# A two-layer hybrid decoder step on one core: the small mixer matmuls rewritten to fill the 128x128 array

## The chip, the cores and the metric

The kernel runs on one core of a Trainium2 chip. The metric is the device time of one execution in microseconds. TensorE multiplies matrices (a stationary operand of weights is loaded, a moving operand streams through) and writes PSUM; VectorE and ScalarE do elementwise work; GpSimd here copies and clears small pieces and issues some of the DMAs; SyncE issues the rest.

## The reference

Two layers. Each runs a half-step SwiGLU FFN, a mixer, and a second FFN, on 256 prompt tokens (one sequence) and 32 sample tokens (8 sequences of 4 tokens, each with a state of its own), 288 columns together. A token is 1024 wide.

The mixer projects with `w_in` and runs three branches side by side: retention (4 heads), HGRN2 (8 heads) and RG-LRU; each is normed, gated, projected, gated again and summed. The two that the change touches are:

```
retention: o_t = sum_{s<=t} gamma^(t-s) (q_t . k_s) v_s + (decayed q_t) S_0 ;  S_new = gamma^n S_0 + sum (decayed k_s)^T v_s
HGRN2:     S_t = diag(f_t) S_{t-1} + k_t^T v_t ,  k = 1 - f ,  o_t = S_t^T q_t        (state 128 x 128 per head)
```

Prompt tokens start from a zero state, sample tokens from the given ones. Outputs are the tokens and all new states.

## The kernel before, in words

Everything is held transposed: features on the 128 partitions, the 288 tokens along the columns (256 prompt, the second half reversed, then 32 sample).

**Gemms.** All weights stream in as tiles of 8 x 128 x 128 (`load_w`, on SyncE's queue, five buffers). `split_w` makes two fp32r tiles of each: `wh` by a ScalarE copy, `wl` by a VectorE subtraction. `gemm` (lines 244 to 250) then runs three fp32r matmuls of 288 columns per block: wh x high part, wh x low part, wl x high part. `next_w` keeps up to three units split ahead. A unit has 24 matmuls.

**Mixer.** `PLAN` is a list, written by hand, of which gemm unit comes when. The heads are generators: each `yield` ends a step, and `pump` runs steps of up to two HGRN heads (or one retention head) after each unit, at 1.65 steps a unit. The framework's scheduler then orders instructions on every engine at compile time, by priority and by when it reckons that operands and buffers are free; on the chip each engine follows its list in order. So the small matmuls of the heads stand between gemm matmuls.

**An HGRN head** (`hgrn_head`). Three transposes bring v to token order (`stack_v`). The score matrix `at` over the prompt tokens is built from its diagonal and then by doubling: at half-widths 1, 2, 4, ..., 64 (`LEVELS`), the later half of each block meets the earlier half of it, and q and k are multiplied by the decay of a half (L682, L683).
- Diagonal: two 128x128 products (L636), and one of 32x32 tokens for the samples (L637), masked by the identity (L640, L643).
- Half-widths 1 to 16: `kc` gathers k (ScalarE), one 128x128 product (L670), a masked copy into `at` (L671). At 1 and 2 a further product of 32 stationary columns for the samples (L677), a masked copy into `ats` (L679), and decays on the sample columns (L688, L689).
- Half-width 32: four products of 32 columns each into four strips of partitions; half-width 64: two of 64 (L664). Each is followed by a ScalarE copy into `at`.
- Samples against their states (`sample_mm`): state tiles `st` come by GpSimd's DMA queue (L631, three buffers) and are split into fp32r halves; `qm` holds q block-diagonally (one buffer, cleared once at the start), and 16 fp32r matmuls of 64 stationary columns (L609, L612) accumulate, with one 32x32 fp32 product of the sample scores among them (L611). `sample_out` copies the 64 rows; `fold`, a 64x32 matrix, adds their halves (L710).
- `po` = v x scores (L708, L709), k to token order, the prompt's new state (L731), and the samples' new states: `km` is k masked per sequence (L621), eight matmuls of 128 columns (L739), eight VectorE updates (L742).

**A retention head** (`ret_head`) is alike, with one dense score block (L830, L831, samples L832), two value halves, two state tiles (L820), a mask from DRAM (`dm`, L823), and two folds (L851).

`norms` (L400) multiplies squares by a 128x128 matrix of ones: the sum over partitions appears on all of them.

Of the kernel before, what the change touches and what calls it, by code (L numbers as in the profile page):

```python
# [12 lines left out]
F32 = mybir.dt.float32  # L13
# [37 lines left out]
LEVELS = (1, 2, 4, 8, 16, 32, 64)  # L51

# [47 lines left out]
def tile_hybrid(ctx: ExitStack, tc, i, o):  # L100
# [73 lines left out]
    dsamp = const("dsamp", (TS, RH, TS))  # L174
    lmask = const("lmask", (P, 4, P))
    smask = const("smask", (TS, 2, 16))
# [6 lines left out]
    fold = const("fold", (64, TS))  # L183
    qms = []
    for j in range(1):
        qm = cp.tile([P, NB * 68], F32R, name=f"qm{j}")
        nc.gpsimd.memset(qm.bitcast(F32), 0.0)
        qms.append(qm)
    qmi = [0]
# [240 lines left out]
    def mixer(l, nx):  # L430
# [141 lines left out]
        def replicate(z):  # L572
            zr = small([P, 96], tag="zrep", bufs=3)
# [11 lines left out]
        def stack_v(z, zr, vT, vs, v1):  # L585
            pt = tokens(z, zr)
            act(vT, pt[:, : 2 * P].rearrange("p (c d) -> p c d", c=2), AF.Copy)
            act(vs, pt[:TS, 2 * P : 3 * P], AF.Copy)
# [3 lines left out]
        def sample_q(qs):  # L592
            qm = qms[0]
# [4 lines left out]
            
# [4 lines left out]
        def sample_mm(pq, j, sp, ats, vs):  # L603
            qm = qms[0]
            dv = slice(j * P, (j + 1) * P)
            for b in range(NB):
# [12 lines left out]
        def bmasked(k1):  # L619
            km = small([96, NB, P], F32R, tag="km", bufs=1)  # L620
            tt(km, k1.bitcast(F32).unsqueeze(1).broadcast_to((96, NB, P)),  # L621
# [4 lines left out]

        def hgrn_head(h, f, k, q, qt, zv, zr):
            vT, vs = vtiles()
# [3 lines left out]
            stack_v(zv, zr, vT, vs, v1)  # L632
            pd = mixps()
            for c in range(2):
                b0 = c * P
# [3 lines left out]
            ats = small([TS, TS], tag="ats", bufs=3)  # L639
# [3 lines left out]
            tt(ats, pd[:TS, TP:T], ident[:TS, :TS], ALU.mult)  # L643
# [3 lines left out]
            for li, hw in enumerate(LEVELS):  # L647
                if hw > 1:
                    yield
                if hw == 2 * DS:  # L650
                    pq = mixps()
                    sample_mm(pq, 0, sp, ats, vs)
                    os_ = sample_out(pq, P)
                w = T if hw < DS else TP
# [4 lines left out]
                pl = mixps()  # L659
                if hw >= 32:  # L660
                    for b in range(nb):
                        s0, c = b * hw, b % 2
                        t0 = s0 - hw if c else s0 + hw
                        mm(pl[s0 : s0 + hw, :hw], k[:, c * P + s0 : c * P + s0 + hw],  # L664
                           qt[:, c * P + t0 : c * P + t0 + hw], start=True, stop=True)
                        act(at[s0 : s0 + hw, c * TP + t0 : c * TP + t0 + hw], pl[s0 : s0 + hw, :hw], AF.Copy)
                else:
                    kc = small([P, P], tag="kc", bufs=1)
                    act(kc.rearrange("p (n c j) -> p n c j", c=2, j=hw), kv, AF.Copy)
                    mm(pl[:, :P], kc, qv, start=True, stop=True)  # L670
# [3 lines left out]
                        pl[:, :P].rearrange("p (n c j) -> p n c j", c=2, j=hw))  # L674
                if hw < DS:
                    rv = qt[:, TP:].rearrange("p (n u j) -> p n u j", u=2, j=hw)[:, :, 1, :]
                    mm(pl[:TS, P : P + 16], k[:, TP:], rv, start=True, stop=True)  # L677
                    av = ats.rearrange("p (n u j) -> p n u j", u=2, j=hw)[:, :, 1, :]
                    nc.vector.copy_predicated(  # L679
                        av, smask[:, li, :].rearrange("p (n j) -> p n j", j=hw).bitcast(U32),  # L680
# [446 lines left out]
```

## Time and profile before

| | |
|---|---|
| time, median of 3 runs | 1956.81 us (1953.67 to 1957.28) |
| span of the profiled execution, first to last instruction | 1951.3 us |
| TensorE matmul, busy | 1922.3 us (99%), 14456 instructions |
| TensorE weight load, busy | 1859.4 us (95%) |
| VectorE | 1343.6 us (69%), 2532 instructions |
| ScalarE | 1095.2 us (56%), 1987 instructions |
| GpSimd | 78.7 us (4%) |
| granted TensorE clock | 0.998 of full speed |
| DMA moved | 318.40 MB, mean 163 GB/s |

The profiled execution has no other time than its span; what lies around the span is the distance to the median of the runs, 5.5 us. How to read it: engines run beside each other, so the busy times don't add up. Ends of matmuls are modelled and overlap, so that the distance between starts tells more than a duration. A line such as L664 is a line of the kernel before; `mix` is a PSUM tile of the mixer, `acc` one of a gemm, `w` a general work tile.

### The profile page before, as it was taken

To read this page: it belongs to the slowest core of one execution; us is meant where nothing else is said; L and a number is where in the kernel's file an instruction comes from. 1 tells how busy PE (TensorE), PEld (TensorE's weight loads), DVE (VectorE), ACT (ScalarE), POOL (GpSimd) and SP (SyncE) were. 2 spreads that over 40 slices of the span, in tenths; PEclk is the share of its full clock that TensorE was granted. 3 is DMA by queue.
4 is the path that set the end of the run, shared out by engine and by line. 5 is a ranking of instruction groups with operands and counts; after the bars stand their busy time and mean duration, and the time that the engine had idled before them with its cause. 6 is when DMAs were issued, how large, how long until landed. Compare 5 with 4: busy or idle time off the path is not lost.

```text
span 1951.3 us, 36645 instructions
## 1 busy us (share of the span) xinstructions
PE 1922.3 (99%) x14456; PEld 1859.4 (95%) x14456; DVE 1343.6 (69%) x2532; ACT 1095.2 (56%) x1987; POOL 78.7 (4%) x206
## 2 busy tenths in 40 slices
PE   8999999999999999999999999999999999999998
PEld 7999998999999999999999999899999999999997
DVE  6665678776677767665566657787766776776654
ACT  7444487656665565444444445775657646654443
POOL 2000022000000000000000001210000000000000
PEclk9999999999999999999999999999999999999999
DMA  7555445635544455555555554445355444555553
GB/s 268 164 167 162 144 143 177 202 112 184 199 143 157 137 189 164 163 171 159 168 171 164 165 165 151 166 153 175 133 185 182 141 137 139 170 166 163 169 163 94
DMA packets 94875, 318.40 MB, mean 163 GB/s; under 512 B 11280, under 2 KB 17360, under 8 KB 94704
## 3 DMA queue, kind: packets, MB, share of 16 engines
q1 hardware_dynamic: 87552, 293.74, 47.0%
q0 software_dynamic: 6576, 21.73, 3.3%
q8 instruction: 114, 1.87, 0.4%
q10 hardware_dynamic: 576, 0.59, 0.1%
q14 instruction: 57, 0.47, 0.1%
HBM read 295.67 MB, written 20.35 MB: 162 GB/s over the span
## 4 chain that ended last, share of the span: by engine, by line
PE 91%; DVE 4%; ACT 3%; issue 1%; POOL 1%; DMA 0%; SPq 0%; DVEq 0%; POOLq 0%; ACTq 0%
PE acc L248 22%; PE acc L249 22%; PE acc L250 22%; PE acc L350 5%; PE acc L351 5%; PE acc L349 5%; PE mix L670 1%; PE mix L664 1%; ACT wh L123 1%; PE mix L612 1%; DVE wl L234 1%; ACT chunk L123 1%; PE mix L609 1%; PE mix L581 1%; PE mix L400 1%
## 5 line engine op out<-in xcount | busy, mean ns | idle before, releaser
L248 PE MATMUL acc<-chunk,wh 128*128 128x288 f32 x3456 | 1037.8, 300 | 8.8 <-ACT wh L123 6.6
L249 PE MATMUL acc<-chunk,wh 128*128 128x288 f32 x3456 | 1024.1, 296 | 0.0
L250 PE MATMUL acc<-chunk,wl 128*128 128x288 f32 x3456 | 1019.1, 295 | 2.4 <-DVE wl L234 2.4
L123 ACT ACTIVATE wh<-wr 128x1024 fp32r<-128x1024 f32 (+2 forms) x531 | 553.1, 1042 | 718.9 <-PE acc L249 357.1
L234 DVE TENSOR_TENSOR wl<-wr,wh 128x1024 fp32r<-128x1024 f32 (+2 forms) x531 | 637.7, 1201 | 264.4 <-ACT wh L123 247.8
L248 PEld LDWEIGHTS acc<-chunk,wh 128*128 128x128 f32 x3456 | 650.2, 188 | 13.0 <-ACT wh L123 8.9
L250 PEld LDWEIGHTS acc<-chunk,wl 128*128 128x128 f32 x3456 | 649.6, 188 | 4.9 <-DVE wl L234 4.1
L249 PEld LDWEIGHTS acc<-chunk,wh 128*128 128x128 f32 x3456 | 650.3, 188 | 3.5 <-DVE chunk L263 0.3
L349 PE MATMUL acc<-chunk,wh 128*128 128x288 f32 x704 | 206.9, 294 | 0.0
L350 PE MATMUL acc<-chunk,wh 128*128 128x288 f32 x704 | 206.9, 294 | 0.0
L351 PE MATMUL acc<-chunk,wl 128*128 128x288 f32 x704 | 206.9, 294 | 0.0
L350 PEld LDWEIGHTS acc<-chunk,wh 128*128 128x128 f32 x704 | 132.1, 188 | 0.0
L351 PEld LDWEIGHTS acc<-chunk,wl 128*128 128x128 f32 x704 | 132.1, 188 | 0.0
L349 PEld LDWEIGHTS acc<-chunk,wh 128*128 128x128 f32 x704 | 132.1, 188 | 0.0
L123 ACT ACT_TABLE_LOAD x84 | 107.8, 1283 | 2.2 <-PEq L1116 0.7
L335 DVE TENSOR_TENSOR z<-acc,rstd 128x288 f32<-128x288 f32 x88 | 40.2, 457 | 73.3 <-PE acc L250 73.3
L332 DVE TENSOR_TENSOR z<-acc,rstd 128x288 f32<-128x288 f32 x88 | 40.2, 457 | 44.8 <-PE acc L250 44.7
L123 ACT ACTIVATE chunk<-z 128x288 fp32r<-128x288 f32 x120 | 53.0, 443 | 16.7 <-DVE z L929 8.8
L682 DVE TENSOR_TENSOR w<-w,w 128x128 f32<-128x128 f32 x112 | 37.4, 334 | 16.6 <-PE mix L664 16.5
L336 DVE TENSOR_TENSOR z<-z,z 128x288 f32<-128x288 f32 x88 | 40.3, 458 | 9.9 <-ACT z L123 1.3
L211 DVE TENSOR_TENSOR sl<-st,sh 128x512 fp32r<-128x512 f32 x64 | 42.1, 684 | 3.5 <-ACT sh L123 3.2
L123 ACT ACTIVATE at<-mix 32x32 f32<-32x32 f32 (+2 forms) x112 | 23.0, 205 | 33.9 <-PE mix L664 33.3
(203 smaller groups left out, 1739.0 us busy)
## 6 DMA issues: line engine op xcount, KB each, us to landing
wr<-in_wmx SPq DMA_DIRECT2D x256, 512.0 KB, 3.6
wr<-in_wgu SPq DMA_DIRECT2D x175, 512.0 KB, 3.5
wr<-in_wd SPq DMA_DIRECT2D x64, 448.0 KB, 3.3
wr<-in_wd SPq DMA_DIRECT2D x32, 512.0 KB, 3.5
st<-in_state_ret POOLq DMA_DIRECT2D x16, 512.0 KB, 5.6
st<-in_state_hgrn POOLq DMA_DIRECT2D x16, 512.0 KB, 5.2
out_ret_s<-st SPq DMA_DIRECT2D x16, 512.0 KB, 3.5
out_hgrn_s<-st SPq DMA_DIRECT2D x16, 512.0 KB, 2.8
```

Of the source, the lines that this page charges most:

```text
L123: r = nc.scalar.activation(out, src, func, **kw)
L211: tt(lo, raw, hi.bitcast(F32), ALU.subtract)
L234: tt(wl[:, k, :], rv, wh[:, k, :].bitcast(F32), ALU.subtract)
L248: mm(ps, wh[:, k, :], xh[k0 + k], start=st, stop=False)
L249: mm(ps, wh[:, k, :], xl[k0 + k], start=False, stop=False)
L250: mm(ps, wl[:, k, :], xh[k0 + k], start=False, stop=sp)
L332: tt(zg, pg[:, :T], rstd, ALU.mult)
L335: tt(zu, pu[:, :T], rstd, ALU.mult)
L336: tt(zu, zu, zg, ALU.mult)
L349: mm(ps[:, :T], wh[:, j, :], a, start=kk == 0, stop=False)
L350: mm(ps[:, :T], wh[:, j, :], b, start=False, stop=False)
L351: mm(ps[:, :T], wl[:, j, :], a, start=False, stop=kk == NF - 1)
```

## The change

- Half-widths 32 and 64 are done like the smaller ones: `kc` is gathered and one 128x128 product made; the four or two ScalarE copies take their blocks from it.
- The diagonal of the scores, half-width 1 and all sample scores no longer come from products on TensorE that are then masked. VectorE multiplies k and q elementwise into a tile `pr` (288 columns for the diagonal, 128 for half-width 1, 24 + 16 + 8 for sample tokens at distance 1, 2 and 3), and one matmul with the ones matrix sums all 464 columns over the partitions. The sample scores stand then on all partitions, and `oi`, their product with v, is made by VectorE and added to the output.
- Half-width 1's `kc` gather, `ats`, `smask` and L611 are gone in HGRN. Retention's sample product moves to `po`, with 96-row operands.
- `fold` and `os` get 128 rows, the lower 64 zero; GpSimd clears them and `qm`, which has two buffers now, for each head.
- The samples' state update masks v instead of k (`vm`), so that k is stationary once and two matmuls of 512 columns take the place of eight of 128.
- An HGRN head has one step more (a `yield` ahead of the ones matmul). The scratch of dynamic DMAs is set to 8192 bytes.

```diff
-    fold = const("fold", (64, TS))
-        qm = cp.tile([P, NB * 68], F32R, name=f"qm{j}")
-        nc.gpsimd.memset(qm.bitcast(F32), 0.0)
+    fold = const("fold", (P, TS))
         def sample_q(qs):
-            qm = qms[0]
+            qm = small([P, NB * 68], F32R, tag="qm", bufs=2)
+            nc.gpsimd.memset(qm.bitcast(F32), 0.0)
...
         def sample_mm
                 mm(pq[:64, dv], qb, sh[:, b % 4, :], start=b == 0, stop=False)
-                if b == NB - 1:
-                    mm(pq[:TS, dv], ats, vs, start=False, stop=False)
                 mm(pq[:64, dv], qb, sl[:, b % 4, :], start=False, stop=b == NB - 1)
         def sample_out(pq, w):
-            os_ = small([64, 2 * P], tag="os", bufs=2)
-            act(os_[:, :w], pq[:64, :w], AF.Copy)
+            os_ = small([P, 2 * P], tag="os", bufs=2)
+            nc.gpsimd.memset(os_[64:, :w], 0.0)
+            act(os_[:64, :w], pq[:64, :w], AF.Copy)
...
+        def pairs(a, off, d):
+            return free(a, TP + off, (DS, NB), (1, DS - d))
         def hgrn_head(h, f, k, q, qt, zv, zr):
+            tt(pr[:, :T], k, q, ALU.mult)
+            tt(pr[:, T : T + P].rearrange("p (n c j) -> p n c j", c=2, j=1), qv, kv, ALU.mult)
+            for d in range(1, DS):
+                w = NB * (DS - d)
+                po = PR_S[d]
+                tt(pr[:, po : po + w].rearrange("p (b t) -> p b t", b=NB), pairs(k, 0, d), pairs(qt, d, d), ALU.mult)
+                tt(pairs(qt, d, d), pairs(qt, d, d), pairs(f, 0, d), ALU.mult)
+            for d in range(1, DS):
+                tt(pairs(k, 0, d), pairs(k, 0, d), pairs(f, d, d), ALU.mult)
+            tt(fp, free(f, TP, (DS, NB), (2, 2)), free(f, TP + 1, (DS, NB), (2, 2)), ALU.mult)
+            tt(tot4, fp[:, :, 0], fp[:, :, 1], ALU.mult)
+            qm = sample_q(qt[:, TP:])
+            sp = split_s(st)
+            yield
             pd = mixps()
-            for c in range(2):
-                mm(pd[:, b0 : b0 + P], k[:, b0 : b0 + P], q[:, b0 : b0 + P], start=True, stop=True)
-            mm(pd[:TS, TP:T], k[:, TP:], q[:, TP:], start=True, stop=True)
+            mm(pd[:, :PR], ones, pr, start=True, stop=True)
-            tt(ats, pd[:TS, TP:T], ident[:TS, :TS], ALU.mult)
+            tt(oi, pd[:, TP:T], zr[:, :TS], ALU.mult)
...
+                if hw == 1:
+                    pl = pd[:, T : T + P]
+                else:
+                    pl = mixps()[:, :P]
+                    act(kc.rearrange("p (n c j) -> p n c j", c=2, j=hw), kv, AF.Copy)
+                    mm(pl, kc, qv, start=True, stop=True)
                 if hw >= 32:
                     for b in range(nb):
-                        mm(pl[s0 : s0 + hw, :hw], k[:, c * P + s0 : c * P + s0 + hw],
-                           qt[:, c * P + t0 : c * P + t0 + hw], start=True, stop=True)
-                        act(at[s0 : s0 + hw, c * TP + t0 : c * TP + t0 + hw], pl[s0 : s0 + hw, :hw], AF.Copy)
+                        act(at[s0 : s0 + hw, c * TP + t0 : c * TP + t0 + hw], pl[s0 : s0 + hw, s0 : s0 + hw], AF.Copy)
...
-                if hw < DS:
-                    mm(pl[:TS, P : P + 16], k[:, TP:], rv, start=True, stop=True)
-                    nc.vector.copy_predicated(
+                if 1 <= li < DS:
+                    tt(tm, prs[:, ps_ - T - P : ps_ - T - P + w].rearrange("p (b t) -> p b t", b=NB), vs[:, :, : DS - li], ALU.mult)
+                    tt(ov[:, :, li:], ov[:, :, li:], tm, ALU.add)
+                if hw == 1:
+                    act(prs, pd[:, T + P : PR], AF.Copy)
...
+            tt(oh[h][:, TP:], po[:, TP:T], oi, ALU.add)
-            km = bmasked(k1)
+            vm = bmasked(v1)
-                for b in range(4):
-                    mm(pu[:, b * P : (b + 1) * P], km[:, 4 * g + b, :], v1, start=True, stop=True)
+                mm(pu, k1, vm[:, 4 * g : 4 * g + 4, :].rearrange("p b d -> p (b d)"), start=True, stop=True)
         def ret_head
-            mm(psc[:TS, 384 : 384 + TS], k[:, TP:], q[:, TP:], start=True, stop=True)
+            mm(psc[:96, 384 : 384 + TS], kr, q[:, TP:], start=True, stop=True)
-                mm(po[:, TP:T], os_[:, dv], fold, start=True, stop=True)
+                mm(po[:, TP:T], vv[j][1], ats, start=True, stop=False)
+                mm(po[:, TP:T], os_[:, dv], fold, start=False, stop=True)
...
+    nc = _bacc.Bacc("TRN2", target_bir_lowering=False, num_devices=1, dynamic_dma_scratch_size=8192)
```

## Rows read from the trace of the kernel before

**Rows 1.** The chain that ended last, shares of the span by engine.
```profile
PE 91%; DVE 4%; ACT 3%; issue 1%; POOL 1%; DMA 0%; SPq 0%; DVEq 0%; POOLq 0%; ACTq 0%
```

**Rows 2.** Windows: length, busy PE, PEld, DVE, ACT, POOL (instructions), PEclk, DMA share, GB/s.
```profile
236.00:345.00 109.00, 104.35 (x754) 96.08 (x754) 91.57 (x190) 85.46 (x195) 25.24 (x75) 1.00 0.47 152
345.00:705.00 360.00, 359.48 (x2736) 338.37 (x2736) 254.13 (x598) 214.95 (x455) 9.57 (x18) 1.00 0.49 162
440.00:460.00 20.00, 20.00 (x153) 19.57 (x152) 17.88 (x39) 10.68 (x29) 2.68 (x5) 1.00 0.63 212
```

**Rows 3.** Timeline of TensorE (start us, length us, instruction, count), around L670.
```profile
637.73 0.29 PE L248 MATMUL acc<-chunk,wh 128*128 128x288 f32 x1
...
637.99 0.29 PE L250 MATMUL acc<-chunk,wl 128*128 128x288 f32 x1
638.12 0.38 PE L670 MATMUL mix<-w,kc 128*128 128x128 f32 x2
...
638.47 0.29 PE L249 MATMUL acc<-chunk,wh 128*128 128x288 f32 x1
```

**Rows 4.** Timeline of TensorE, around one 32-column product.
```profile
642.54 0.29 PE L250 MATMUL acc<-chunk,wl 128*128 128x288 f32 x1
642.76 0.25 PE L664 MATMUL mix<-w,w 128*32 128x32 f32 x2
...
643.18 0.29 PE L249 MATMUL acc<-chunk,wh 128*128 128x288 f32 x1
```

**Rows 5.** Timeline of TensorE, around one 64-column product.
```profile
622.14 0.29 PE L248 MATMUL acc<-chunk,wh 128*128 128x288 f32 x1
622.36 0.33 PE L664 MATMUL mix<-w,w 128*64 128x64 f32 x2
...
622.86 0.29 PE L250 MATMUL acc<-chunk,wl 128*128 128x288 f32 x1
```

**Rows 6.** Timeline of TensorE, end of one head's sample matmuls.
```profile
394.88 0.22 PE L612 MATMUL mix<-sl,qm 128*64 128x128 f32 x1
394.94 0.22 PE L609 MATMUL mix<-sh,qm 128*64 128x128 f32 x1
395.10 0.40 PE L611 MATMUL mix<-vs,ats 32*32 32x128 f32 x2
395.43 0.27 PE L612 MATMUL mix<-sl,qm 128*64 128x128 f32 x1
```

**Rows 7.** Timeline of TensorE, an HGRN head's opening products (L636, L637, L670).
```profile
396.14 0.61 PE L636 MATMUL mix<-w,w 128*128 128x128 f32 x4
...
397.42 0.30 PE L249 MATMUL acc<-chunk,wh 128*128 128x288 f32 x1
```

**Rows 8.** Timeline of TensorE, a retention head's L849, L850, L851, twice.
```profile
355.15 0.59 PE L849 MATMUL mix<-at,vT 128*128 128x256 f32 x2
...
357.66 0.30 PE L249 MATMUL acc<-chunk,wh 128*128 128x288 f32 x1
```

**Rows 9.** Timeline of TensorE, four norms.
```profile
433.84 2.15 PE L400 MATMUL mix<-w,ones 128*128 128x288 f32 x8
...
435.96 0.30 PE L249 MATMUL acc<-chunk,wh 128*128 128x288 f32 x1
```

**Rows 10.** Timeline of TensorE, half of a head's state update.
```profile
646.57 0.56 PE L739 MATMUL mix<-v1h,km 96*128 96x128 f32 x4
...
647.15 0.30 PE L249 MATMUL acc<-chunk,wh 128*128 128x288 f32 x1
```

**Rows 11.** VectorE by line and shape: busy us, mean ns, idle before, releaser.
```profile
L765 DVE TENSOR_TENSOR w<-w,w 128x288 f32<-128x288 f32 x16 | 7.3, 454 | 0.1
...
L688 DVE TENSOR_TENSOR w<-w,w 128x16 f32<-128x16 f32 x32 | 5.0, 158 | 0.0
```

**Rows 12.** GpSimd by line; and its waits: us in total, times, longest.
```profile
L187 POOL MEMSET qm<- 128x544 f32 x1 | 0.6, 570 | 0.0
...
POOL st L820 <- DVE k L720: 124.6, 2, 62.4
```

More of the change, by code (lines that the diff above doesn't have):

```diff
@@ L51 @@
 LEVELS = (1, 2, 4, 8, 16, 32, 64)
+PR_S = {1: T + P, 2: T + P + 24, 3: T + P + 40}
+PR = T + P + 48
 C_QR, C_KR, C_VR, C_GR = 0, 4, 8, 16
@@ L572, in replicate @@
         def replicate(z):
-            zr = small([P, 96], tag="zrep", bufs=3)
+            zr = small([P, 96], tag="zrep", bufs=5)
             act(zr.rearrange("p (r t) -> p r t", r=3),
@@ L587, in stack_v @@
             act(vT, pt[:, : 2 * P].rearrange("p (c d) -> p c d", c=2), AF.Copy)
-            act(vs, pt[:TS, 2 * P : 3 * P], AF.Copy)
+            if vs is not None:
+                act(vs, pt[:96, 2 * P : 3 * P], AF.Copy)
             act(v1, pt[:96, 2 * P : 3 * P], AF.Copy)
@@ L625, in mixer @@
         oh = {}
+        def pairs(a, off, d):
+            return free(a, TP + off, (DS, NB), (1, DS - d))
         def hgrn_head(h, f, k, q, qt, zv, zr):
-            vT, vs = vtiles()
+            vT = small([P, 2, P], tag="vT", bufs=5)
             v1 = small([96, P], F32R, tag="v1h", bufs=3)
@@ L642, in hgrn_head @@
                ident.unsqueeze(1).broadcast_to((P, 2, P)), ALU.mult)
-            tt(ats, pd[:TS, TP:T], ident[:TS, :TS], ALU.mult)
+            oi = small([P, TS], tag="oi", bufs=3)
+            vs = zr[:, :TS].rearrange("p (b t) -> p b t", b=NB)
+            ov = oi.rearrange("p (b t) -> p b t", b=NB)
+            tt(oi, pd[:, TP:T], zr[:, :TS], ALU.mult)
             tot = f
@@ L658, in hgrn_head @@
                 kv = free(k, 0, dims[0], (P + hw, 2), dims[1])
-                pl = mixps()
+                if hw == 1:
+                    pl = pd[:, T : T + P]
+                else:
+                    pl = mixps()[:, :P]
+                    kc = small([P, P], tag="kc", bufs=1)
+                    act(kc.rearrange("p (n c j) -> p n c j", c=2, j=hw), kv, AF.Copy)
+                    mm(pl, kc, qv, start=True, stop=True)
                 if hw >= 32:
@@ L710, in hgrn_head @@
             mm(po[:, TP:T], os_[:, :P], fold, start=True, stop=True)
+            oh[h] = chunks(F32, 1)[0]
+            tt(oh[h][:, TP:], po[:, TP:T], oi, ALU.add)
+            act(oh[h][:, :TP], po[:, :TP], AF.Copy)
             sq = small([P, T], tag="w", bufs=WB)
[L712 to L714 removed]
+            act(sq, oh[h], AF.Square)
             pt = tokens(k, kr)
@@ L919, in vtiles @@
         def vtiles():
-            return small([P, 2, P], tag="vT", bufs=5), small([TS, P], tag="vs", bufs=5)
+            return small([P, 2, P], tag="vT", bufs=5), small([96, P], tag="vs", bufs=4)
         def do_g(br, cg, oo, n):
@@ L1031, in shape_constants @@
     ok = (a[:, None] // DS == a[None, :] // DS) & (a[None, :] >= a[:, None])
-    dsamp = np.stack([np.where(ok, np.exp(g * np.maximum(a[None, :] - a[:, None], 0)) * scale, 0.0) for g in lg], 1)
+    dsamp = np.zeros((96, RH, TS))
+    dsamp[:TS] = np.stack([np.where(ok, np.exp(g * np.maximum(a[None, :] - a[:, None], 0)) * scale, 0.0) for g in lg], 1)
     qdec = np.broadcast_to(np.stack([np.exp(g * (a % DS + 1.0)) for g in lg], 0)[None], (P, RH, TS))
@@ L1039, in shape_constants @@
     lm = np.stack([p[:, None] // hw == p[None, :] // hw for hw in LEVELS[1:5]], 1)
-    sm = np.zeros((TS, 2, 16))
-    for li, hw in enumerate(LEVELS[:2]):
-        c = np.arange(16)
-        later = (c // hw) * 2 * hw + hw + c % hw
-        sm[:, li, :] = (a[:, None] // (2 * hw) == later[None, :] // (2 * hw)) & (a[:, None] % (2 * hw) < hw)
     ident = np.eye(P)
-    fold = (np.arange(64)[:, None] % TS == np.arange(TS)[None, :]).astype(np.float32)
-    out = dict(fold=fold, cosc=cosc, sinc=sinc, dmask=dmask, dsamp=dsamp, lmask=lm, smask=sm, ident=ident,
+    fold = np.zeros((P, TS))
+    fold[:64] = np.arange(64)[:, None] % TS == np.arange(TS)[None, :]
+    out = dict(fold=fold, cosc=cosc, sinc=sinc, dmask=dmask, dsamp=dsamp, lmask=lm, ident=ident,
                qdec=qdec, kdec=kdec, kdecs=kdecs, bmask=bmask)
```

70 lines of the change are left out of this document (25 added, 45 removed).

## The prediction, made before the changed kernel was run

> **What bounds the kernel now.** I read the chain of waits first [rows 1]: 91% of the span is TensorE, 4% VectorE, 3% ScalarE, and DMA rounds to 0%. Then the windows of the first layer's mixer [rows 2], where all edits lie; the second layer repeats it about 960 us later. From 345 to 705 us TensorE is busy for 359.48 of 360 us, VectorE for 254.13 (71%), ScalarE for 214.95 (60%), GpSimd for 9.57. TensorE sets the pace, and a busy TensorE need not be a useful one. So I read its timeline last, for one quantity: how much later the gemm goes on because a small matmul was put into it. In an undisturbed gemm matmuls of 288 columns start 0.13 us apart (637.73 to 637.99 are two steps, [rows 3]). The price of an inserted group is the time from the gemm matmul before it to the second one after it, less two steps of 0.13; where the group starts its 0.13 after the gemm, from its own start, less one step.
>
> - A full 128x128 product (L670, two instructions, as each fp32 matmul has) costs 638.47 - 638.12 - 0.13 = 0.22 us [rows 3].
> - A 32-column one (L664 at half-width 32), a quarter of the weights and a quarter of the columns, costs 643.18 - 642.54 - 0.26 = 0.38 us, and the rows show part of it as a pause: 0.22 instead of 0.13 before it starts [rows 4].
> - A 64-column one costs 622.86 - 622.14 - 0.26 = 0.46 us [rows 5].
> - The 32x32 product inside the sample matmuls (L611) puts 0.49 us between two neighbours that otherwise start 0.06 apart: 0.43 us [rows 6]. Those neighbours, 64 columns of fp32r, show no such gap, and the change keeps them.
>
> So the narrow fp32 tiles cost more than the wide ones, with a pause that the wide ones don't have.
>
> **The change, term by term (TensorE).** Two layers of eight HGRN heads make 16, two of four retention heads 8.
>
> Removed per HGRN head:
> - Opening diagonals (L636, two full), sample diagonal (L637, 32 columns), level 1 (L670): 397.42 - 396.14 - 0.13 = 1.15 us [rows 7].
> - Two sample matmuls at levels 1 and 2 (L677), the same 128x32 tile as L664: 2 x 0.38 = 0.76.
> - Level 32: four at 0.38 = 1.52. Level 64: two at 0.46 = 0.92.
> - L611: 0.43.
> - The 64-row fold. In a retention head, where the same trio stands twice, (357.66 - 355.15 - 0.13) / 2 = 1.19 us [rows 8]. Two of the trio are full tiles of 256 + 128 columns. For columns: four norm matmuls of 288 columns cost 435.96 - 433.84 - 0.13 = 1.99, 0.50 each, 1.73 ns a column [rows 9]. 384 columns are 0.66, the fold 0.53.
> - State update, eight matmuls: 2 x (647.15 - 646.57 - 0.13) = 2 x 0.45 = 0.90 [rows 10].
>
> Sum: 6.21 us.
>
> Added per HGRN head: one matmul with ones over PR = 464 columns, 464 x 1.73 ns = 0.80; one full product each at levels 32 and 64, 0.44; the 128-row fold, 0.22; two state matmuls of 512 fp32r columns, by the gemm step 512/288 x 0.13 = 0.23 each, 0.46. Sum 1.92. Net 4.29 x 16 = 69 us.
>
> Per retention head: out go L832 (0.38), two L611 (0.86), two folds (1.06), 2.30 in all; in come the 96-column score, two 96-row sample products and two folds, five at no more than a full product, 1.10. Net 1.20 x 8 = 10 us.
>
> Together 79 us. Unknown is what a full tile with only 32 moving columns costs (no row has one outside the narrow modes): at most the 0.22 of 128 columns, at least half of it, 0.11, what one of the four 96x128 matmuls in [rows 10] costs. That concerns 16 folds and 40 retention products, 56 x 0.11 = 6 us more gain at the far end. I take 0.22, since its weights are as wide as those of the 0.22 row.
>
> **A rule weighed.** The row says that a narrow tile costs 0.38 against 0.22 for a full one [rows 3, 4]. The Trainium skill, TensorEngine Tiling (Array Packing), section Overview, puts it the other way: a product with a small dimension up to 32 leaves the full array idle, and narrow tiles are worth up to four times as much. By that the four products of level 32 would cost what one full one does and the two of level 64 likewise, the merging would bring nothing, and 16 x (1.52 + 0.92 - 0.44) = 32 us would leave the sum: 47 us. The trace does not agree: one tile at a time, between full ones, shows no concurrency to win.
>
> **What moves to the other engines.** VectorE per HGRN head gains the k·q product over 288 columns (0.454), the strided level-1 product over 128 (priced like the former, 0.454, since strided reads may cost more), and 19 tiny ones (six for sample pairs, three for k, two for totals, one diagonal, six at levels 2 to 8, one closing add); it loses seven (L643, two L679, four of L688/689). 12 x 0.158 + 0.91 = 2.8 us net [rows 11], 45 us in all on an engine that was idle for 29% of the stretch. ScalarE is close to even: it loses level 1's kc copy and the HGRN vs copy, and gains one copy of 48 columns. GpSimd gains a memset of qm per head at 0.57 us [rows 12], and a smaller one for os; 24 of each are under 28 us on a queue that is almost always idle. These cost nothing as long as VectorE still delivers wl in time. Its cover: three units of split weights, 3 x 24 x 0.13 = 9 us of gemm.
>
> That cover thins. The stretch 345 to 705 holds seven HGRN and three retention heads. It shrinks to 360 - 7 x 4.29 - 3 x 1.20 = 326 us, and VectorE's work grows to 254 + 7 x 2.8 = 274 us: 84%. That is the share of the stretch 236 to 345 (91.57 of 109), in which TensorE idles 4.65 us, 4.3% [rows 2]. At that rate 14 us a layer are given back, 28 in all; at the present rate of the later stretch (0.52 of 360) nothing is. Against the high end: the early stretch also has ScalarE at 78%, the later one at 60%, and in 440 to 460 us VectorE was at 89% while TensorE did not idle at all [rows 2]. I take 4 us a layer, 8 in all, nearer to that low end. The next thing late is then wl, not a mixer operand.
>
> **Sum.** 1951.3 - 79 + 8 = 1880 us of span. The span lies 5.5 us under the median of the three runs (1956.8); with the same 5.5 the time is 1886 us, 71 less.
>
> **Rivals.**
> 1. *VectorE becomes the mixer's bound.* The 28 us are given back in full: 1951.3 - 79 + 28 + 5.5 = 1906. For it: 84% in a dependent mix of work. Against it: the 440 to 460 us window.
> 2. *The stalls are not due to the narrow tile, but to being a small dependent insertion,* and the merged products keep the excess. Then only the number of matmuls falls: the fold stays at 0.53, levels 32 and 64 cost 0.38 + 0.46, retention gains nothing: 16 x (4.29 - 0.31 - 0.40) = 57 us, or 1951.3 - 57 + 8 + 5.5 = 1908. For it: L664 waits on ScalarE's copies. Against it: L670 also waits on a fresh ScalarE copy and costs 0.22. The Trainium skill, TensorEngine Tiling (Array Packing), section Tiling Modes, has a change of tiling mode drain the engine; the trace agrees with its pause ahead of the tile.
> 3. *VectorE hardly matters and 32 moving columns are cheap*: 1951.3 - 85 + 5.5 = 1872.
> 4. *Slower: the new memsets get caught in GpSimd's queue.* That queue waits at its head for a state buffer (L820, up to 62.4 us, twice) [rows 12]. A qm memset queued behind such a load is late by that much. Behind the memset stands ScalarE's copy into qm, behind that copy ScalarE's weight copies, and TensorE runs dry after its 9 us of cover: 2 x (62.4 - 9) = 107 us lost against 79 won, 1951.3 - 79 + 107 + 5.5 = 1985. It decides from the point where a memset is queued after a load whose buffer comes free later than the head needs qm. For it: in the retention head the memset is issued after both state loads and the mask load. Against it: the head needs that mask load one step later in the kernel before as well, and its products show no wait for it; the scheduler places a load when its buffer is free by its own reckoning, so memsets of earlier heads stand ahead of it.
>
> **How the numbers follow.** Forecast, 1876 to 1898: 0.52. Rival 3, below 1876: 0.16. Rivals 1 and 2, 1898 to 1912: 0.22 (0.17 and 0.05). Something between there and no change: 0.05. Rival 4: 0.05. The range 1867 to 1908 holds the forecast, nearly all of rival 3 and most of rivals 1 and 2. Under 0.2% (3.9 us) no measurement of this kernel tells a change from none. Faster: 0.52 + 0.16 + 0.22 + 0.03 = 0.93; the remaining 0.02 of the middle case I put within 0.2%; slower 0.05.
>
> **What would show it.** Right: no fp32 matmul of 32 or 64 columns is left, and every gap of a gemm at a mixer matmul falls to full-tile size; L664's merged product costs 0.22; the ones matmul 0.80; windows of TensorE shorter by 4.3 us per HGRN head; VectorE's share in the mixer around 84%. Wrong: gemm matmuls that wait for VectorE's wl for more than a few us (rival 1), gaps around the 128-column products (rival 2), or ScalarE idle until a GpSimd memset (rival 4). The prediction fails if TensorE's idle time in the mixers grows by more than some 25 us, or if a full-tile product with few columns costs much over 0.22.

## The result: 33 us less, where 71 were forecast

The changed kernel takes 1923.96 us (median of 4 runs, 1921.35 to 1927.71), the kernel before 1957.05 beside it: ratio 0.9829, 95% interval 0.9811 to 0.9847. That is 33 us less; the forecast was 1886, and the time lies above the range's end of 1908. The profiled execution has a span of 1921.5 us and a time of 1923.3.

The chain of waits of after, shares of the span by engine, answers to [rows 1]:

```profile
PE 77%; DVE 10%; ACT 8%; DMA 2%; issue 2%; POOL 0%; SPq 0%; DVEq 0%; ACTq 0%; POOLq 0%
```

The windows of after, with the columns of [rows 2]:

```profile
236.00:345.00 109.00, 101.91 (x741) 95.30 (x740) 94.20 (x208) 86.12 (x196) 30.32 (x79) 1.00 0.48 147
345.00:705.00 360.00, 346.78 (x2661) 336.59 (x2661) 274.05 (x715) 228.67 (x481) 17.98 (x39) 1.00 0.54 172
```

TensorE was busy for 359.48 of the 360 us of the later stretch; now it idles for 13.22 of them, and for 7.09 instead of 4.65 us of the earlier one. From its first to its last matmul it idles for 47 us in all, where it was 15: the growth of 32, of which the first layer's two stretches hold 15, is more than the 25 in the mixers that the prediction named as a sign of its failure. The work has become cheaper, and TensorE waits for it. VectorE's share is 76%, not the 84% forecast.

The prices came out as worked. TensorE's timeline of after, around a ones matmul and a merged product, at a fold, and around half a state update:

```profile
613.30 0.94 PE L651 MATMUL mix<-pr,ones 128*128 128x464 f32 x2
614.08 0.38 PE L680 MATMUL mix<-w,kc 128*128 128x128 f32 x2
614.22 0.38 PE L243 MATMUL acc<-chunk,wh 128*128 128x288 f32 x1
614.43 0.30 PE L244 MATMUL acc<-chunk,wh 128*128 128x288 f32 x1
...
590.44 0.31 PE L718 MATMUL mix<-c_fold,os 128*128 128x32 f32 x2
590.58 0.42 PE L576 MATMUL mix<-c_ident,w 128*128 128x128 f32 x2
...
598.18 0.40 PE L747 MATMUL mix<-km,k 96*128 96x512 f32 x1
598.41 0.30 PE L243 MATMUL acc<-chunk,wh 128*128 128x288 f32 x1
598.55 0.30 PE L244 MATMUL acc<-chunk,wh 128*128 128x288 f32 x1
```

The ones matmul costs 614.08 - 613.30 = 0.78 us (forecast 0.80), the full product 614.43 - 614.08 - 0.13 = 0.22 (0.22), the state matmul 598.55 - 598.18 - 0.13 = 0.24 (0.23). The fold, a full tile with 32 moving columns, for which the prediction had only the bounds 0.11 and 0.22, takes 590.58 - 590.44 = 0.14. All mixer matmuls of the trace, each form times the price of its undisturbed rows, come to 261 us before and 185 after: 76 us less, where the prediction had 79. These sums are estimates. The gemm is the same in both (12480 steps of some 0.1313, 1639 us). What is left of TensorE's time between its first and last matmul, the waits and slow stretches, is 37 us before and 84 after. So the price term held, and **some 43 us were given back instead of 8** (76 priced, 33 measured).

Where: what TensorE waits for in after (line waited at, releaser: us in total, times, longest):

```profile
PE acc L243 <- ACT wh L125: 7.4, 2, 5.1
PE mix L680 <- DVE w L700: 7.2, 6, 2.4
PE mix L680 <- ACT kc L125: 5.2, 8, 1.1
...
PE acc L243 <- ACT chunk L125: 3.2, 2, 1.6
...
PE mix L747 <- DVE km L616: 3.0, 2, 1.5
PE mix L680 <- ACT w L125: 3.0, 2, 1.5
...
PE acc L245 <- DVE wl L229: 2.7, 5, 1.0
```

What grew are not the waits for split weights (`wl`: 2.7 us in all, 2.4 before; `wh`: 7.4, 6.6 before) but those for mixer operands, above all of the 128x128 products of the half-widths (L680, merged ones among them). And what ScalarE waits for in after:

```profile
ACT prs L125 <- DVE at L687: 16.9, 12, 2.9
ACT qm L125 <- DVE w L643: 15.9, 10, 4.0
```

Two copies hold ScalarE's queue for 33 us. The one into `qm` takes the samples' q once the last of VectorE's tiny products is made; the one into `prs` takes the 48 sample sums out of the ones matmul's PSUM tile, and its wait ends with VectorE's masked copy (L687) from the same tile. In the kernel before, the copy into `qm` waited for HGRN's VectorE for 1.7, and there was no `prs`. The worst place, as the timeline of after has it (start, length, instruction, [idle before <- releaser]):

```profile
574.65 0.39 DVE L643 TENSOR_TENSOR w<-w,w 128x24 f32<-128x24 f32 x2
...
574.83 0.23 ACT L125 ACTIVATE qm<-w 128x32 fp32r<-128x32 f32 x1 [4.04 <-DVE w L643]
...
574.97 1.14 ACT L125 ACTIVATE sh<-st 128x512 fp32r<-128x512 f32 x2
...
575.62 1.29 DVE L206 TENSOR_TENSOR sl<-st,sh 128x512 fp32r<-128x512 f32 x2 [0.25 <-ACT sh L125]
...
576.01 1.04 ACT L125 ACTIVATE wh<-wr 128x1024 fp32r<-128x1024 f32 x1
576.83 1.11 DVE L750 SCALAR_TENSOR_TENSOR st<-st,tot,mix 128x128 f32<-128x128 f32 x4
576.96 0.39 ACT L125 ACTIVATE z<-acc 128x288 f32<-128x288 f32 x1
577.25 0.29 ACT L125 ACTIVATE kc<-w 128x128 f32<-128x128 f32 x1
...
578.06 0.28 DVE L700 TENSOR_TENSOR w<-w,w 128x128 f32<-128x128 f32 x1
...
578.49 0.77 PE L680 MATMUL mix<-w,kc 128*128 128x128 f32 x2 [2.35 <-DVE w L700]
```

One head's `qm` copy stands idle for 4.04 us until the run of tiny products ends; behind it in the same queue stand the state and weight splits and the other head's `kc` gather, and TensorE starts the product 2.35 us late. ScalarE is not alone in that: the gather ends at 577.54, and the last operand, VectorE's L700, 0.8 us later. VectorE's queue has the state split `sl`, which waited for ScalarE's `sh`, and four state updates (L750) ahead of it.

### The profile page after: what moved, and what is told of

Its sections match the earlier page's. It is cut to its first block, busy times and chain, and to the rows that moved or that the text cites. A ratio compares the mean times of both kernels' runs of the same rounds, so it can differ in the third digit from the quotient of the medians.

```text
span 1921.5 us, 36168 instructions
## 1 busy us (share of the span) xinstructions
PE 1860.6 (97%) x14040; PEld 1823.3 (95%) x14040; DVE 1364.3 (71%) x2756; ACT 1098.7 (57%) x2005; POOL 103.6 (5%) x252
## 4 chain that ended last, share of the span: by engine, by line
PE 77%; DVE 10%; ACT 8%; DMA 2%; issue 2%; POOL 0%; SPq 0%; DVEq 0%; ACTq 0%; POOLq 0%
PE acc L243 19%; PE acc L244 19%; PE acc L245 19%; PE acc L344 5%; PE acc L346 5%; PE acc L345 5%; DVE wl L229 2%; ACT L125 2%; ACT wh L125 2%; ACT chunk L125 1%; DMA st<-in_state_ret 1%; PE mix L680 1%; DVE sl L206 1%; ACT w L125 1%; DMA wr<-in_wgu 1%
## 5 line engine op out<-in xcount | busy, mean ns | idle before, releaser
L680 PE MATMUL mix<-w,kc 128*128 128x128 f32 x192 | 40.4, 292 | 15.6 <-DVE w L700 7.2
L680 PEld LDWEIGHTS mix<-w,kc 128*128 128x128 f32 x192 | 30.1, 190 | 21.3 <-ACT kc L125 14.3
```

The lines of the kernel that those rows point to most:

```text
L680: mm(pl, kc, qv, start=True, stop=True)
```

## The experiments

Three theories were stated at first. A: ScalarE's queue is held by copies that wait for VectorE's new products. B: VectorE has too much work. C: TensorE's order, fixed at compile time, leaves operands no slack once its work is short. Each table line gives the time against the kernel before run beside it, the priced saving (an estimate, from 261 us, as above), what was given back (priced saving less measured saving), and the theories in whose expected range the time lies ("none": outside all of them). Theories D to F came later: D, the run of tiny products ahead of the other head's decays; E, the prompt's diagonal and half-width 1; F, any VectorE work there. The kernel before had medians of 1956.41 to 1959.89 in these rounds; where two kernels of different rounds are compared, the difference of their medians and the difference of their savings can therefore lie some 3 us apart, and both are given where they do.

| kernel | median us | ratio, 95% interval | priced | given back | in the range of |
|---|---|---|---|---|---|
| the change | 1923.96 | 0.9829 [0.9811, 0.9847] | 76 | 43 |  |
| levels_only | 1939.17 | 0.9909 [0.9893, 0.9924] | 32 | 15 | C |
| pe_only | 1917.36 | 0.9797 [0.9780, 0.9813] | 53 | 14 | none |
| pe_dummy | 1921.15 | 0.9813 [0.9798, 0.9827] | 53 | 18 | A, C |
| fix_all | 1920.84 | 0.9815 [0.9800, 0.9829] | 76 | 40 | B, C |
| products_only | 1971.97 | 1.0066 [1.0051, 1.0081] | 23 | 35 | none |
| products_dve | 1953.92 | 0.9984 [0.9974, 0.9993] | 23 | 20 | none |
| qm_dve | 1909.85 | 0.9749 [0.9735, 0.9764] | 76 | 26 | none (0.85 above A) |
| pe_qm | 1913.85 | 0.9783 [0.9768, 0.9797] | 53 | 10 | A |
| pe_kc | 1912.09 | 0.9762 [0.9744, 0.9779] | 53 | 5 | none |
| after_kc | 1924.06 | 0.9821 [0.9804, 0.9839] | 76 | 40 | none (0.06 above A) |
| qm_dve_kc | 1909.75 | 0.9763 [0.9748, 0.9777] | 76 | 29 | the rival |
| pe_kc_qm | 1909.82 | 0.9762 [0.9747, 0.9777] | 53 | 5 | A |
| spread | 1911.07 | 0.9765 [0.9750, 0.9779] | 74 | 27 | E, F |
| samp_dve | 1895.93 | 0.9694 [0.9677, 0.9710] | 74 | 13 | D, E |
| samp_pool | 1896.37 | 0.9691 [0.9677, 0.9705] | 74 | 13 | D, E |
| samp_yield | 1914.24 | 0.9778 [0.9762, 0.9794] | 74 | 30 | none (2 above the step) |
| samp_diag | 1906.03 | 0.9739 [0.9724, 0.9753] | 75 | 22 | E |
| samp_diag_ny | 1888.89 | 0.9651 [0.9635, 0.9667] | 75 | 5 | none (6 below the step) |

**Parts of the change, VectorE's load, a first repair.** levels_only merges half-widths 32 and 64 in the kernel before; pe_only adds the 128-row fold, the two state matmuls and retention's 96-row scores, but no VectorE products; pe_dummy adds 17 VectorE products per HGRN head that nobody reads; fix_all moves three places of the changed kernel. This diff and those below are cut to the lines that tell the edit.

```diff
 levels_only against the kernel before (pe_only has this too)
                 if hw >= 32:
+                    act(kc.rearrange("p (n c j) -> p n c j", c=2, j=hw), kv, AF.Copy)
+                    mm(pl[:, :P], kc, qv, start=True, stop=True)
-                        mm(pl[s0 : s0 + hw, :hw], k[:, c * P + s0 : c * P + s0 + hw],
-                           qt[:, c * P + t0 : c * P + t0 + hw], start=True, stop=True)
 pe_only against levels_only (and the fold and retention as in the change)
-            km = bmasked(k1)
+            km = bmasked(v1)
-                    mm(pu[:, b * P : (b + 1) * P], km[:, 4 * g + b, :], v1, start=True, stop=True)
+                mm(pu, k1, km[:, 4 * g : 4 * g + 4, :].rearrange("p b d -> p (b d)"), start=True, stop=True)
 pe_dummy against pe_only
+            for e in range(17):
+                tt(par2[:, 5, :], negc, posc, ALU.mult)
 fix_all against the change
-            qm = sample_q(qt[:, TP:])        # step 0, before the ones matmul
-            sp = split_s(st)
+                if hw == 2:                  # where it was before
+                    qm = sample_q(qt[:, TP:])
+                    sp = split_s(st)
-                if hw == 1:                  # prs copy, now right behind the ones matmul
-            tt(oh[h][:, TP:], po[:, TP:T], oi, ALU.add)
-            act(sq, oh[h], AF.Square)
+            act(sq[:, :TP], po[:, :TP], AF.Square)
+            tt(oh[h][:, TP:], po[:, TP:T], oi, ALU.add)
+            tt(sq[:, TP:], oh[h][:, TP:], oh[h][:, TP:], ALU.mult)
```

> The kernel before with one edit: half-widths 32 and 64 as one full product each (kc, 128x128) in place of four and two narrow ones. By the prices of the prediction 16 x (1.52 + 0.92 - 0.44) = 32 us less: 1925 us. Theory A (ScalarE's in-order queue is held up by copies that wait for VectorE's new products, so later operands come late to TensorE): no such copy is added, so the 32 us come in full, 1920 to 1930, and TensorE's idle time stays near the 15 us of before. Theory B (VectorE has too much work): no work is added, the same. Theory C (the order on TensorE was laid out for slower matmuls; once they are quick, operands are late whatever made them): a third to a half is given back, 1936 to 1942, with 10 us more idle.

> The kernel before with the parts of the change that add nothing to VectorE: merged half-widths 32 and 64, the 128-row fold, the state update as two matmuls of 512 columns, and retention's sample scores with 96 rows. The diagonal and HGRN's sample scores stay on TensorE as before. By the prices 32 + 7 + 5 + 10 = 54 us less: 1903 us. A and B: 1898 to 1910, idle up by under 8 us. C: more than a third is given back, 1920 to 1930, idle up by 20 us or more.

> As pe_only, with 17 tiny VectorE products of 16 columns per HGRN head that nobody reads (17 x 0.16 = 2.7 us, what the change adds net). They are put in one row after the head's first masked copies. B: VectorE's share alone gives time back, 12 us or more over pe_only. A: nobody waits for them, within 5 us of pe_only, but for what the row of them delays behind it. C: within 5 us of pe_only.

> The changed kernel with the three new waits of ScalarE on VectorE taken out, at the same work: the copy into qm (and the state split) goes back to half-width 2, where the kernel before had it; the copy of the 48 sample columns (prs) comes straight after the ones matmul, ahead of VectorE's reads of that bank; the output copy and its square no longer stand behind the closing add (VectorE squares the 32 sample columns). A: TensorE's idle time falls from 47 us to some 25 and the time to 1900 to 1908. B: the work is the same, 1918 to 1925. C: 1915 to 1925.

levels_only gives back 15 of its 32 us without any new product, as C has it; pe_only lies between the ranges of A and C. The matmul edits alone are faster than the whole change: the products part, priced at 23 us, costs 7. Seventeen idle products cost 3.8 us, so B explains little. fix_all missed A's range and brought 3 us. No wait of the `prs` copy is left in its trace, so those 16.9 us of ScalarE were worth no more than that. It did not test the other one: the `qm` copy still waits 17.2 us in 11 places. At the worst of them it stands at the same point of ScalarE's order as in after, and again idles 4.04 us.

**ScalarE's queue.** products_only is the kernel before with the products part alone; the added step comes with it, and so do the change's scratch size and its five `zrep` buffers (three before). qm_dve is the change with the two copies made by VectorE, which makes the products too; products_dve is products_only with the same, pe_qm the control: pe_only with its `qm` copy moved, where no run of products stands ahead of it.

```diff
 products_only against the kernel before (with pr's products, oi and tm as in the change)
-                mm(pd[:, b0 : b0 + P], k[:, b0 : b0 + P], q[:, b0 : b0 + P], start=True, stop=True)
-            mm(pd[:TS, TP:T], k[:, TP:], q[:, TP:], start=True, stop=True)
+            mm(pd[:, :PR], ones, pr, start=True, stop=True)
 qm_dve against the change, products_dve against products_only, pe_qm (first pair only)
-            act(qd[:, :, 0:DS], q3, AF.Copy)
+            nc.vector.tensor_copy(qd[:, :, 0:DS], q3)
-                    act(prs, pd[:, T + P : PR], AF.Copy)
+                    nc.vector.tensor_copy(prs, pd[:, T + P : PR])
 and, but for pe_qm, the last lines of fix_all
```

> The kernel before with the products part alone: diagonal, half-width 1 and all sample scores of the HGRN heads from VectorE's products and one ones matmul; half-widths 32 and 64, the fold, the state update and retention stay as before. By the prices of the prediction it takes 16 x (1.15 + 0.76 + 0.43 - 0.80) = 25 us off TensorE. Theory A (ScalarE's queue is held up by copies that wait for the new products, whatever TensorE's pace): all of it is given back, 1953 to 1960, and the late TensorE products are those fed by ScalarE. Theory C (any shortening of TensorE's work makes operands late, since the order is laid out at compile time for slower matmuls): about half is given back, as where half-widths 32 and 64 were merged alone (32 priced, 17 gained): 1940 to 1947. Prices alone: 1932.

> The changed kernel, with the two small copies that made ScalarE wait for the new products (q into qm, the 48 sample sums into prs) made by VectorE instead, which computes the products itself, and with the square of the head's output no longer behind the closing add. ScalarE then waits for none of the tiny products. Theory A: ScalarE's waits on them (16 + 17 us in the trace of after) are what makes the merged products late (18 us at their line); 15 to 30 us come back, 1894 to 1909. Theory C: ScalarE's waits move elsewhere, less than 6 us come back, 1918 to 1924.

> The kernel with the products part alone (it took 1972 us, 12 more than before), with the copies into qm and prs made by VectorE and the square of the output not behind the closing add. Theory A: the loss was ScalarE's queue standing behind the products; without those waits the 25 us of the prices show at least by half, 1932 to 1948, faster than before. Theory B' (VectorE's extra products themselves are what makes operands late): moving two more copies to VectorE brings nothing, 1966 to 1976.

> Control: the kernel with the matmul edits alone (1917 us, no new products), with the copy into qm made by VectorE. There ScalarE waits for VectorE at this copy for 9.6 us in all, longest 1.8. Theory A (what counts is the wait behind a long run of products): less than 6 us come back, 1911 to 1918. Rival (any copy taken off ScalarE gives that much, products or not): 10 or more come back, 1903 to 1908.

products_only is slower than before, and ScalarE waits in it as in after:

```profile
ACT prs L125 <- DVE at L694: 15.8, 12, 2.7
ACT qm L125 <- DVE w L648: 10.5, 4, 4.0
```

Without these waits 18 us come back (1971.97 to 1953.92; 15 by the savings), in the changed kernel 14 (1923.96 to 1909.85; 17 by the savings), though VectorE has more to do in both; in the control 3.5. A is shown for that much, with one reserve: the moved square of the output is in both numbers, at no more than the 3 us of fix_all. A missed the number in products_dve (1932 to 1948 expected), so some 20 of 23 us were still given back for another reason.

**The gather one step earlier.** pe_kc, after_kc, qm_dve_kc and pe_kc_qm issue the `kc` gather of the next half-width at the end of the step before (three buffers); the latter two have the copies on VectorE as well. pe_kc also has the scratch size of the change, which pe_only lacks.

```diff
-                    kc = small([P, P], tag="kc", bufs=1)
-                    act(kc.rearrange("p (n c j) -> p n c j", c=2, j=hw), kv, AF.Copy)
+                if hw < 64:                  # at the end of a step, bufs=3
+                    kc = gather(k, 2 * hw)
```

> The kernel with the matmul edits alone (1917 us), with one thing moved: the kc gather of the next half-width is issued at the end of the step before it, in three buffers instead of one, so that a step of the head lies between the gather and its product. Theory C (the dependent chain decay, gather, product has no slack once TensorE is quick): most of the lateness at the kc products goes, 8 to 18 us come back, 1899 to 1909. Theory A: nothing here waits for new VectorE products, so nothing comes back, 1914 to 1919.

> The changed kernel with the same move: the kc gather one step ahead of its product, three buffers. Theory C: the 18 us by which the merged products came late go, and some of what follows from them, 1896 to 1908. Theory A: the gather still stands behind the copies into qm and prs on ScalarE's queue, less than 6 us come back, 1918 to 1924.

> The changed kernel with both moves: copies into qm and prs by VectorE (alone 1910 us) and the kc gather one step ahead of its product (alone 1924 us, nothing). Theory A: the early gather could not help as long as ScalarE stood behind the products; now it gives what it gave without them (5 us), 1902 to 1907. Rival (the early gather gives nothing where VectorE has the products): 1908 to 1913.

> The matmul edits alone with both moves (gather ahead alone: 1912 us). Theory A: the two are independent and small, 1907 to 1912. By the prices the changed kernel with both moves should be 23 us under this one; by what has been measured so far the two are about level, as the products give back most of what they save.

C has 5 us in the kernel without products (9 by the savings; 8 to 18 were expected) and nothing clear of the noise in the changed one, with or without ScalarE's waits: qm_dve_kc is level with qm_dve, as the rival had it, and A missed. In pe_kc_qm the two moves together bring 7.5 us, alone 5.3 and 3.5; whether they add up is within the noise.

**The burst, or the prompt's scores.** spread is qm_dve with the eleven sample products broken up: one distance per step, a ones matmul of their own at half-width 4. samp_dve is pe_kc_qm with only the sample scores as products, spread in that way; diagonal and half-width 1 stay three full products. samp_pool has their work on GpSimd.

```diff
 spread against qm_dve (pair(d): the product and the decay of q at distance d)
-            for d in range(1, DS):
+            pair(1)
             yield
+                if hw == 1:
+                    pair(2)
+                if hw == 2:
+                    pair(3)
+                    qm = sample_q(qt[:, TP:])
+                    if hw == DS:
+                        mm(pf[:, P : P + 48], ones, ps, start=True, stop=True)
 samp_dve against pe_kc_qm
-            mm(pd[:TS, TP:T], k[:, TP:], q[:, TP:], start=True, stop=True)
+            st_(ps[:, :TS], k[:, TP:], q[:, TP:], ALU.mult)
+            pair(1)                          # pair(2), pair(3) one step later each
-                    mm(pl[:TS, P : P + 16], k[:, TP:], rv, start=True, stop=True)
+                if hw == DS:
+                    mm(pl[:, P : P + 80], ones, ps, start=True, stop=True)
-                    mm(pq[:TS, dv], ats, vs, start=False, stop=False)
 samp_pool against samp_dve (and the copy into qm)
-    st_ = nc.vector.tensor_tensor
+    st_ = nc.gpsimd.tensor_tensor
```

> The changed kernel with the copies into qm and prs on VectorE (1910 us), and the sample products no longer in one run of eleven: one distance per step, their 48 columns summed by a ones matmul of their own at half-width 4 (some 0.1 to 0.2 us a head, 2 to 3 us in all), the additions at half-widths 16 and 32. The number of VectorE instructions is the same. Theory D (the burst ahead of the other head's decays): 8 to 18 us come back, 1892 to 1902. Theories E and F: nothing comes back, 1909 to 1914.

> The matmul edits alone with both moves (1910 us), and of the products part the sample scores only: 80 columns of products made by VectorE, spread over the steps, summed by one ones matmul at half-width 4; diagonal and half-width 1 stay full matmuls, and no step is added. By the prices it takes 16 x (0.38 + 0.76 + 0.43 - 80 x 1.73 ns) = 23 us off. Theory E (the loss sits in diagonal and half-width 1): most of that shows, 1887 to 1896. Theory D: likewise, as the burst is gone. Theory F (any VectorE work there gives it back): 1904 to 1912.

> The same with the sample work (products, decays, copy into qm, additions) on GpSimd, which was nearly idle. If VectorE's load is what gives the time back (theory F), it is faster than the one with VectorE, 1887 to 1896; by theories D and E it is level with it or slower, as GpSimd's chain of small instructions is longer and what waits for it (qm, prs) comes later: 1888 to 1905.

The burst theory (D) falls: spread is 1.2 us behind qm_dve. The sample scores keep 14 of the 21 us that the table prices, on VectorE and on GpSimd alike, so neither the products as such nor VectorE's load take it back. What samp_dve lacks beside qm_dve is the prompt's products and the added `yield`.

**The added step.** samp_yield is samp_dve with one more `yield` ahead of the head's opening matmuls and nothing else. samp_diag has the prompt's products and their ones matmul with the step, samp_diag_ny without it.

```diff
 samp_yield against samp_dve
+            yield
             pd = mixps()
             for c in range(2):
 samp_diag against samp_dve (samp_diag_ny: the same without the yield)
+            tt(pr[:, :TP], k[:, :TP], q[:, :TP], ALU.mult)
+            tt(pr[:, TP:].rearrange("p (n c j) -> p n c j", c=2, j=1), qv, kv, ALU.mult)
+            yield
             pd = mixps()
-            for c in range(2):
-                mm(pd[:, b0 : b0 + P], k[:, b0 : b0 + P], q[:, b0 : b0 + P], start=True, stop=True)
+            mm(pd[:, : TP + P], ones, pr, start=True, stop=True)
```

> The best kernel so far (samp_dve, 1896 us) with the prompt's diagonal and half-width 1 done as in the change: two VectorE products (256 and 128 columns), one more step, one ones matmul of 384 columns in place of three full products. By the prices 384 x 1.73 ns = 0.66 against 0.66 us: no change, 1894 to 1899. Theory E (the loss of the change sits here): 8 to 16 us slower, 1904 to 1912.

> The same without the added step. If the products and the longer link are what costs, as slow as samp_diag or slower, 1904 to 1915, the ones matmul waiting for the fresh products. If the added step is what costs, 1895 to 1900.

> samp_dve (1896 us) with the added step alone: an HGRN head yields once more ahead of its opening matmuls, nothing else is changed. If the step is what costs (heads last longer against the units of gemm that cover them): 1903 to 1912. If the products cost: 1894 to 1899.

The step is it: 18.3 us without the products (1895.93 to 1914.24; 17.2 by the savings), 17.1 with them (1888.89 to 1906.03). The products themselves gain 7 or 8 us, where the prices said nothing. samp_diag alone would have spoken for E; without the step the same products are the fastest of all. The table bears it out: each of the ten kernels that have the added step gives back some 20 us or more, and none of the nine without it more than 18. products_dve has it too; there it would be nearly all of the 20 us left open, though it was not taken out of that kernel. TensorE's waits in samp_dve, then in samp_yield:

```profile
PE mix L614 <- DVE sl L212: 4.1, 6, 0.9
...
PE mix L689 <- ACT kc L124: 2.7, 4, 0.9
...
PE acc L249 <- ACT chunk L124: 0.8, 2, 0.4
```

```profile
PE mix L690 <- DVE w L703: 5.5, 5, 1.9
PE acc L249 <- ACT chunk L124: 5.0, 4, 1.7
...
PE mix L775 <- DVE km L624: 3.2, 2, 1.6
PE mix L690 <- ACT w L124: 3.2, 2, 1.6
...
PE mix L614 <- DVE sl L212: 2.3, 4, 0.9
...
PE mix L690 <- ACT kc L124: 1.3, 2, 0.7
```

Both issue the same 14136 matmuls and 2796 VectorE instructions; the same products (L689 of one is L690 of the other) come late by 10.0 instead of 2.7 us. All waits of TensorE together grow by some 11 us, where the two spans differ by 15.7 (1893.0 and 1908.7); the rest isn't placed. One such place, first in samp_dve, then in samp_yield:

```profile
645.11 0.43 PE L689 MATMUL mix<-w,kc 128*128 128x128 f32 x2
...
645.61 2.10 PE L401 MATMUL mix<-w,ones 128*128 128x288 f32 x8
645.91 1.28 ACT L124 ACT_TABLE_LOAD   x1
647.20 1.68 ACT L124 ACTIVATE w<-mix,eps 128x288 f32<-128x288 f32 x4
```

```profile
655.24 2.10 PE L401 MATMUL mix<-w,ones 128*128 128x288 f32 x8
...
656.40 1.28 ACT L124 ACT_TABLE_LOAD   x1
...
658.22 1.28 ACT L124 ACT_TABLE_LOAD   x1
659.52 1.67 ACT L124 ACTIVATE w<-mix,eps 128x288 f32<-128x288 f32 x4
660.07 0.49 PE L690 MATMUL mix<-w,kc 128*128 128x128 f32 x2 [1.61 <-ACT w L124]
```

Ahead of the norms (L401) the product stood clear; one step later it stands behind them and is released by ScalarE's reading of their sums, after two table loads. The changed kernel has this very wait (1.50 us at 665.12), and the late `km` and `chunk` of samp_yield too.

**The best version** is samp_diag_ny, 1888.89 us (1888.14 to 1889.19), 35 us under the change. Its windows:

```profile
236.00:345.00 109.00, 104.93 (x784) 99.65 (x783) 97.44 (x219) 88.20 (x198) 29.41 (x79) 1.00 0.51 157
345.00:705.00 360.00, 356.54 (x2769) 349.62 (x2769) 287.07 (x760) 232.52 (x474) 11.53 (x28) 1.00 0.57 178
```

VectorE is busier than in the change (287.07 against 274.05 us) and TensorE idles for 3.46 us instead of 13.22.

## Why the prediction was wrong

- **Prices of the removed and added matmuls: right.** 76 of 79 us, and the three new forms within 0.02 us each. Rival 2 (small insertions keep their stall) falls with the 0.22 of L680. So does what the prediction drew from the Trainium skill (TensorEngine Tiling (Array Packing), Overview), that merging half-widths 32 and 64 would bring nothing: alone it brought 17 us. The page states its speedups for independent tiles, and here one narrow tile ran at a time.
- **"I take 4 us a layer, 8 in all": the step that failed.** It measured 43. It was sized by VectorE's share of the time, with `wl` as what would be late next. VectorE's share came out lower than forecast, its busy time in all grew by 20.7 us (1343.6 to 1364.3) instead of 45, `wl` waits stayed at 2.7 us, and the best version has a higher share and less idle time. What came late in its place were mixer operands, for the next two reasons. So rival 1, too, had the wrong mechanism; what it allowed, 28, was too small.
- **"ScalarE is close to even": even in busy time, not in its queue.** The prediction counted the copies' time and asked neither what each waits for nor what stands behind it, which it did ask of GpSimd's queue in rival 4. Worth 14 us in the change (17 by the savings), most of it at the `qm` copy. The Trainium skill (TensorE: Matmul & The Clock Gate, section Architectural detail: the array is 16× 32×32, not 1× 128×128) calls ScalarE's and VectorE's queues strictly first in, first out; the rows at 574.83 to 577.25 agree.
- **The added step was given no price at all.** It stands in the change as one `yield`. It was measured at 17 to 18 us, in samp_dve's surroundings; with the 14 of ScalarE's queue that leaves 43 - 14 - 18 = 11 (43 - 17 - 17 = 9 by the savings), near the 8 of the forecast. That this rest comes out near 8 does not bear out how the 8 were sized. The sum is made across kernels: taking the step alone out of the changed kernel wasn't tried.
- **Rival 4 (memsets caught in GpSimd's queue)** didn't occur: neither TensorE nor ScalarE waits for GpSimd anywhere in after, and ScalarE's wait ahead of `qm` ends on VectorE's L643.
- **The forecast's own range, 1876 to 1898,** holds samp_dve, samp_pool and samp_diag_ny, which have the same matmul savings (74 to 75 us) without the two mishaps. The chain's DMA, 2% now, is for nearly half state tiles of retention (20 of 44 us), which ScalarE's split waits for, and for the rest the program's first loads and stores of states; it wasn't pursued. Still open is why levels_only gives back 15 of 32 us; the early gather (5 us in pe_kc) may be a part of it, which wasn't tried there. Other numbers of steps weren't tried, so 18 us is what this step costs against this plan, not what a step costs.

## What to carry to other kernels

Price a removed instruction by the gap it leaves in the busy engine's timeline; that came within 4% here, estimate against estimate. But the price is paid out only if every in-order queue still delivers: for each new copy, name what it waits for and what stands behind it, and give a copy of fresh products to the engine that makes them. A change of the order in a hand-placed schedule, even an empty step, is an edit of its own: time it apart from the work that it carries.

## What was not expected of the hardware

A late operand can cost more than its wait. After the 2.35 us of idle that end at 578.49 the granted clock fell to half, the lower of its two levels; the windows of after:

```profile
578.50:580.50 2.00, 2.00 (x9) 2.00 (x10) 2.00 (x7) 1.06 (x5) 0.00 (x0) 0.50 0.17 63
580.50:582.50 2.00, 2.00 (x13) 2.00 (x13) 0.45 (x2) 0.57 (x1) 0.00 (x0) 0.66 0.92 238
582.50:584.50 2.00, 2.00 (x18) 2.00 (x17) 1.69 (x3) 1.95 (x7) 0.53 (x1) 1.00 0.56 225
...
1525.00:1527.00 2.00, 1.95 (x15) 1.98 (x16) 2.00 (x7) 1.07 (x6) 0.00 (x0) 1.00 0.11 45
```

Over these 4 us TensorE ran at 0.50 and 0.66, so 2 x 0.50 + 2 x 0.34 = 1.7 us more were lost to a wait of 2.35. It need not happen: the same wait in the second layer, 2.35 us that end at 1525.05, left the clock at 1.00 (the last window). And some twenty tiny products, decays, additions and copies per head ran as well on GpSimd as on VectorE (1896.37 and 1895.93 us).
